# Refilling the first expert's first weight buffer in two halves, in a mixed attention, convolution and expert layer

## The chip, the cores and the metric

The kernel runs on one core of a Trainium2 chip. Its engines work side by side: TensorE (PE, with weight loads as PEld), VectorE (DVE), ScalarE (ACT), GpSimd (POOL) and SyncE (SP), which issues nearly all transfers from memory. The metric is the device time of one execution in microseconds, lower is better; the times stated are medians of several executions.

## What is computed

The reference is one encoder layer on 512 tokens of width 1024 in float32. The first half (attention heads beside a convolution, then a norm) comes first; the change lies in the second half, the mixture of experts:

```python
def expert_choice_moe(h, w_router, w_gate, w_up, w_down):
    capacity = CAPACITY_FACTOR * S // N_EXPERTS
    logits = jnp.einsum('bsd,de->bse', h, w_router).astype(jnp.float32)
    affinity = jax.nn.softmax(logits, axis=-1)
    gates, idx = lax.top_k(affinity.transpose(0, 2, 1), capacity)
    xg = jax.vmap(lambda hb, ib: hb[ib])(h, idx)
    a = jnp.einsum('becd,edf->becf', xg, w_gate)
    u = jnp.einsum('becd,edf->becf', xg, w_up)
    y = jnp.einsum('becf,efd->becd', jax.nn.silu(a) * u, w_down)
    y = y * gates[..., None].astype(y.dtype)
    ...
```

There are 16 experts, each takes its 64 best tokens (capacity 2 * 512 / 16) and has three weight matrices of 1024 x 2048 numbers, 8 MB each. The weights of all experts, some 400 MB, are read once.

## The kernel before

**Weights and memory.** A chunk is 1 MB of weights (128 rows by 2048). Expert e has 24 chunks: 0 to 7 of w_gate, 8 to 15 of w_up, 16 to 23 of w_down. Chunks live in ten buffers of 2 MB (`b` in the profile, `big_tile`), each of two slots (`s`). The first 22 chunks are loaded while the layer's first half still computes: twenty of them into slots, in the order of `first_chunks`, and chunks 14 and 15 into small tiles (`sq`, `q`) that are not part of the ring. All later chunks come in pairs: `take_big` gives the next buffer of the ring, one transfer of 2 MB fills it (L157, the function `stream`), and it waits until the products that read the buffer's old chunks are done. The first buffer holds chunks 0 and 1 and gets chunks 22 and 23, the second holds 8 and 9 and gets the first two of expert 1, and so on. SyncE issues them in this order.

**The products.** For each expert the loop of L1177 goes through blocks (k, j): k = 0 for w_gate, 1 for w_up, and j = 0 to 3 for two chunks each. Expert 0 goes (0,0), (1,0), (0,1), (1,1), (0,2), (1,2), (0,3), (1,3); the others finish k = 0 first. Within a block x and y give the chunk c = 2j + a and the half b of its columns. One such step is two matmuls in the program and four passes in the trace, since a float32 product runs as two passes; where the row of the trace says x8, that is one chunk. Steps with k = 0 are called slots. After each block `stream` issues one refill (L1249). The (1,3) block of expert 0 reads the small tiles and has no refill behind it. Then come the transposes of the hidden values (L1258) and the down products (`py`, L1287), with a refill after every second chunk.

**Other work among the products.** For expert 0 the gathered tokens `xg` are made on the way. `gather` makes them column by column: eight passes of TensorE into half a PSUM bank (`sg`, L1044), then ScalarE copies them out (L1045, 128x128). Two columns share one tile of PSUM, so columns 2 and 3 do. The loop asks for the next column at the first step of each chunk with k = 0 (L1199). `ranks` works out the places of expert e + 2 in steps taken at every third slot (L1212): a transpose (L238) that VectorE compares into masks (L240), and counts of the masks by TensorE (L245) one step later. TensorE keeps the order in which the program is written; the other engines are ordered by a scheduler.

Of the kernel before, what the change touches and what calls it, by code (L numbers as in the profile page):

```python
# [26 lines left out]
PREFETCH, LATE = 22, 14  # L27
# [19 lines left out]
def layer_kernel(ctx, tc, x, positions, emb_ln_g, emb_ln_b, w_in, q_norm_g, w_qb, kv_norm_g, w_kvb,  # L47
                 conv_w, conv_b, conv_ln_g, conv_ln_b, w_o, ln1_g, ln1_b, w_router,
                 w_gate, w_up, w_down, ln2_g, ln2_b, rope_rows, out):
    nc = tc.nc  # L50
# [22 lines left out]
    def slot(i, dt=F32):  # L73

        if (i, dt) not in handles:
            handles[i, dt] = nc.alloc_sbuf_tensor_at(f"s{len(handles)}", [128, 2048], dt,
                                                     offset=base + place[i] * 8192)
        return handles[i, dt].ap()

    def big_tile(b):  # L80
        if b not in handles:
            handles[b] = nc.alloc_sbuf_tensor_at(f"b{b}", [128, 4096], F32, offset=base + b * 16384)
        return handles[b].ap()

    def quarters(t):
        return [t[:, j * 512:(j + 1) * 512] for j in range(4)]
# [10 lines left out]
    w_tiles = {}  # L97
    next_chunk = [0]
# [4 lines left out]
    def take_big(back=True):  # L103

        b = ring.pop(0)
        if back:
            ring.append(b)
        return big_tile(b)

    def quarter_tile(q, dt=F32):  # L110
        return slots.tile([128, S], dt, name=f"q{q}")
# [4 lines left out]
    def source(i, n):  # L116

        e, r = divmod(i, 24)
        k, c = divmod(r, 8)
        if k < 2:  # L120
            rows = (w_gate, w_up)[k][0, e, c // 2 * 256:c // 2 * 256 + 256, :]
            v = rows.rearrange("(p a) n -> p a n", a=2)
            return v[:, c % 2:c % 2 + n, :]
        rows = w_down[0, e, c // 2 * 512:c // 2 * 512 + 512, :]
        v = rows.rearrange("(p a m) n -> p a (m n)", a=2, m=2)
        return v[:, c % 2:c % 2 + n, :]

    def stream(upto):
        while next_chunk[0] < min(upto, E * 24):

            n = next_chunk[0]
            if n < PREFETCH - 2:
                i = first_chunks[n]
                t = slot(first_ring[n])
                nc.sync.dma_start(t, source(i, 1)[:, 0])
                w_tiles[i] = quarters(t)
                next_chunk[0] += 1
            elif n < PREFETCH:
                i = LATE + n - PREFETCH + 2
                w_tiles[i] = []  # L140
                tiles = [quarter_tile(q) for q in range(4)] if i > LATE else [pair_tile(F32), pair_tile(F32)]
                m = 2048 // len(tiles)
                for q, t in enumerate(tiles):
                    t = t if i > LATE else t.rearrange("p a n -> p (a n)")
                    nc.sync.dma_start(t, source(i, 1)[:, 0, q * m:(q + 1) * m])
                    w_tiles[i] += [t[:, f * 512:(f + 1) * 512] for f in range(m // 512)]
                next_chunk[0] += 1
            else:
                t = take_big().rearrange("p (a n) -> p a n", a=2)
                if n == E * 24 - 2:  # L150

                    src = source(n, 2)
                    for q in range(4):
                        h = slice(q % 2 * D, q % 2 * D + D)
                        nc.sync.dma_start(t[:, q // 2, h], src[:, q // 2, h])
                else:
                    nc.sync.dma_start(t, source(n, 2))  # L157
                for a in range(2):
                    w_tiles[n + a] = quarters(t[:, a])
                next_chunk[0] += 2  # L160


    ints = slot(17, I32)
# [98 lines left out]
    with ExitStack() as pre:  # L262
# [126 lines left out]
        for c in range(DC):  # L389
            p = bank("tr")  # L390
# [149 lines left out]
        for j in range(2):  # L540
            p = project(QR + j * 128)
# [20 lines left out]
        for j in range(3):  # L562
            p = project(j * 128)
# [52 lines left out]
        for r in range(2):  # L616
            e, o = (quarters(slot(4 - 2 * r + s, F32R)) for s in range(2))
# [37 lines left out]
        for i in range(4):  # L655
            p = bank()
# [479 lines left out]
    def ranks(e):  # L1136

        pr = ps.tile([128, 512], F32, name="tr")
        ms = []
        for t in range(TT + 1):  # L1140
            if t:
                count(t - 1, pr[:, 256:256 + TT], ms[t - 1])
            if t < TT:
                ms.append(mask_tile(wk, 2))
                compare(e, t, pr[:, t % 2 * 128:(t % 2 + 1) * 128], ms[t])
            yield
        rank(e, pr[:, 256:256 + TT])

    def step(gen):
        next(gen, None)  # L1150

    hot, chosen = {}, {}
    nothing = iter(())
    ga = gather(0)
    next(ga)
    sc = nr = nothing
    for e in range(E):
# [5 lines left out]
        else:  # L1163

            order = [(k, j) for j in range(DC // 2) for k in range(2)]
        rk = ranks(e + 2) if e + 2 < E else nothing
        if e == 2:
            residual()
        left = slots_seen = 0
# [7 lines left out]
        for k, j in order:  # L1177
            p = pgu[k]
            i = 24 * e + 8 * k + 2 * j
            ws = [w_tiles.pop(i + a) for a in range(2)]  # L1180
            final = k == 1 and j == DC // 2 - 1
            if last and (k, j) == (1, 0):

                py = ps.tile([128, 512], F32, name="py")
                for t in range(TT):
                    for hf in range(2):
                        tensor(nc.tensor.matmul(py[hf * 64:(hf + 1) * 64], hot[E // 2 - 1][:, t, CAP:],
                                         acc[t][:, hf * 512:(hf + 1) * 512], start=t == 0, stop=False))
            if (k, j) == (1, 2) and s and not last:
                ga = gather(pair + 1)  # L1190
                next(ga)
            for x in range(2):
                for y in range(2):

                    a, b = (y, x) if final else (x, y)
                    c = 2 * j + a
                    if e == 0 and k == 0 and b == 0:

                        next(ga, None)  # L1199
                    for g in range(2):  # L1200
                        tensor(nc.tensor.matmul(p[b][g * 64:(g + 1) * 64, :], xg[:, c, s * CAP:(s + 1) * CAP], ws[a][2 * b + g],  # L1201
                                         start=c == 0, stop=c == DC - 1))
                    if last:
                        if k == 0 and y and left:
                            step(sc)
                            left -= 1
                    elif k and not final and left > 1:
                        step(sc)
                        left -= 1
                    elif k == 0:  # L1210
                        if slots_seen % 3 == 0:
                            step(rk)  # L1212
                        slots_seen += 1
                if final:
                    if last:
                        nc.vector.scalar_tensor_tensor(hh[:, x], sg[:, x], gate, p[x], op0=OP.mult, op1=OP.mult)
                    else:
                        nc.vector.tensor_tensor(hh[:, x], sg[:, x], p[x], op=OP.mult)  # L1218
            if (k, j) == (0, DC // 2 - 1):
                sg = pair_tile(F32)  # L1220
                hh = sg
                for b in range(2):
                    nc.scalar.activation(sg[:, b], pgu[0][b], AF.Silu)  # L1223
            if last and (k, j) == (0, DC // 2 - 1):
                nr = norm_rows()
            elif last and k and not final:
                step(nr)
                if j < 2:
                    step(nr)
            if not LATE <= i < LATE + 2:  # L1230

                if (e, k, j) == (1, 1, 3):
                    t4 = take_big(back=False)
                    acc.extend(t4[:, t * D:(t + 1) * D] for t in range(TT))
                elif (e, k, j) == (E - 2, 0, 0):

                    gb2 = take_big(back=False)
                    g2, b2 = gb2[:, :D], gb2[:, D:2 * D]
                    gb2h = quarters(gb2[:, 2 * D:])[:2]
                    spread(g2, 2 * DC, 1.0)  # L1240
                elif (e, k, j) == (E - 2, 0, 1):
                    spread(b2, 3 * DC, 1.0)
                    for dst, src in zip(gb2h, (g2, b2)):
                        for hf in range(2):
                            rs = slice(hf * 64, (hf + 1) * 64)
                            nc.scalar.activation(dst[rs], src[rs, hf * 512:(hf + 1) * 512], AF.Identity)
                    stream(next_chunk[0] + 2)
                else:
                    stream(next_chunk[0] + 2)  # L1249
# [5 lines left out]
        for b in range(2):  # L1255
            p = ps.tile([128, 512], F32, name="sg", bufs=2) if b else ps.tile([128, 512], F32, name="tr")
# [19 lines left out]
        for c in range(8):  # L1276
# [4 lines left out]
            for a in range(2):  # L1281
                f = 2 * c + a
                b, g, j = f // 8, (f // 4) % 2, f % 4
# [65 lines left out]
```

## Time and profile before

| | |
|---|---|
| median of 3 executions | 1198.47 us (1198.46 to 1198.53) |
| profiled execution, its own time | 1197.94 us |
| its span, first to last instruction | 1196.2 us |
| TensorE busy | 1122.5 us, 94% |
| VectorE, ScalarE, GpSimd busy | 380.3, 250.2, 199.3 us |
| chain that ended last | PE 65%, DMA 27% |
| read from memory | 419.60 MB |

The share of an engine is an average over the whole span. Which engine or which transfer sets the end is read from stretches: the expert stage runs from about 277 us to the end. A transfer's issue on SyncE is 0.33 us long in the trace; the data move afterwards, which the rates per stretch show.

### The profile page before, as it was taken

To read this page: it belongs to the slowest core of one execution; us is meant where nothing else is said; L and a number is where in the kernel's file an instruction comes from. 1 tells how busy PE (TensorE), PEld (TensorE's weight loads), DVE (VectorE), ACT (ScalarE), POOL (GpSimd) and SP (SyncE) were. 2 spreads that over 40 slices of the span, in tenths; PEclk is the share of its full clock that TensorE was granted. 3 is DMA by queue.
4 is the path that set the end of the run, shared out by engine and by line. 5 is a ranking of instruction groups with operands and counts; after the bars stand their busy time and mean duration, and the time that the engine had idled before them with its cause. 6 is when DMAs were issued, how large, how long until landed. Compare 5 with 4: busy or idle time off the path is not lost.

```text
span 1196.2 us, 13662 instructions
## 1 busy us (share of the span) xinstructions
PE 1122.5 (94%) x5573; PEld 529.7 (44%) x5573; DVE 380.3 (32%) x901; ACT 250.2 (21%) x461; POOL 199.3 (17%) x234
## 2 busy tenths in 40 slices
PE   4899998999999999999999999989997999899996
PEld 3687775785434343433433343324332433243422
DVE  5799998542110212122012102110311031102241
ACT  4545777322101100100110011001110101012110
POOL 6768567300000600000000000000000000000040
PEclk9899999999999999999999999999999999999998
DMA  6421014777999999999999999999999999999997
GB/s 200 138 74 43 10 68 144 253 279 292 378 425 428 428 425 427 428 428 427 428 427 428 427 427 427 428 427 427 428 428 428 428 427 427 428 427 427 428 427 293
DMA packets 43681, 422.85 MB, mean 353 GB/s; under 512 B 5178, under 2 KB 13187, under 8 KB 18018
## 3 DMA queue, kind: packets, MB, share of 16 engines
q1 hardware_dynamic: 41456, 419.18, 84.5%
q10 hardware_dynamic: 2082, 2.53, 0.6%
q8 instruction: 43, 0.70, 0.2%
q0 software_dynamic: 80, 0.26, 0.1%
q14 instruction: 20, 0.16, 0.0%
HBM read 419.60 MB, written 2.36 MB: 353 GB/s over the span
## 4 chain that ended last, share of the span: by engine, by line
PE 65%; DMA 27%; DVE 4%; ACT 2%; issue 1%; POOL 1%; ACTq 0%; POOLq 0%; SPq 0%; DVEq 0%
PE gu L1201 25%; DMA b<-in_w_up_dram 15%; PE py L1287 15%; DMA b<-in_w_down_dram 9%; PE sg L1044 6%; PE pj L258 4%; PE pj L259 3%; PE pj L260 3%; PE sg L1091 2%; DVE cv L453 1%; PE st L772 1%; ACT s L227 1%; DMA s<-in_w_in_dram 1%; PE tr L1066 1%; DMA s<-in_w_o_dram 1%; PE tr L757 1%
## 5 line engine op out<-in xcount | busy, mean ns | idle before, releaser
L1201 PE MATMUL gu<-b,xg 128*64 128x512 f32 x1920 | 446.5, 600 | 28.8 <-DMA b<-in_w_up_dram 18.1
L1201 PEld LDWEIGHTS gu<-b,xg 128*64 128x64 f32 x1920 | 124.6, 136 | 267.9 <-issue 206.4
L1287 PE MATMUL py<-b,sq 128*64 128x512 f32 x976 | 227.7, 601 | 2.7 <-DMA b<-in_w_down_dram 2.6
L1056 POOL COPY sq<-oh 128x256 f32<-128x256 f32 x16 | 6.0, 402 | 746.2 <-PE sg L1258 746.2
L1287 PEld LDWEIGHTS py<-b,sq 128*64 128x64 f32 x976 | 63.2, 136 | 106.3 <-issue 94.0
L1081 DVE SCALAR_TENSOR_TENSOR q<-py,gates,q 64x512 fp32r<-64x512 f32 x30 | 22.5, 749 | 236.3 <-ACT q L1080 236.3
L1044 PEld LDWEIGHTS sg<-oh,h 128*128 128x128 f32 x512 | 65.3, 197 | 45.5 <-issue 43.8
L258 PE MATMUL pj<-s,s 128*128 128x512 f32 x189 | 77.9, 421 | 7.6 <-ACT q L435 3.2
L1044 PE MATMUL sg<-oh,h 128*128 128x128 f32 x512 | 76.5, 293 | 1.3 <-DVE oh L1035 0.7
L259 PE MATMUL pj<-s,s 128*128 128x512 f32 x189 | 76.8, 407 | 0.0
L1218 DVE TENSOR_TENSOR sq<-sq,gu 128x512 f32<-128x512 f32 x30 | 20.6, 687 | 174.9 <-PE gu L1201 174.9
L1094 DVE TENSOR_TENSOR b<-sg,b 128x512 f32<-128x512 f32 x64 | 43.9, 690 | 83.7 <-PE sg L1091 79.6
L228 POOL TENSOR_TENSOR s<-s,s 128x512 fp32r<-128x512 f32 (+2 forms) x54 | 64.9, 1226 | 19.4 <-ACT s L227 13.0
L1262 ACT ACTIVATE sq<-tr 128x512 f32<-128x512 f32 x16 | 9.6, 597 | 273.3 <-PE tr L1258 273.3
L1045 ACT ACTIVATE xg<-sg,gbp 128x128 f32<-128x128 f32 x64 | 29.3, 458 | 162.9 <-PE sg L1044 162.9
L260 PE MATMUL pj<-s,s 128*128 128x512 f32 x157 | 63.2, 406 | 0.0
L453 DVE SCALAR_TENSOR_TENSOR cv<-s,q,cv 128x512 f32<-128x512 f32 x83 | 62.2, 749 | 1.7
L1223 ACT ACTIVATE sq<-gu 128x512 f32<-128x512 f32 x32 | 18.9, 597 | 190.6 <-PE gu L1201 190.6
L240 DVE SCALAR_TENSOR_TENSOR mask<-tr,aff,ones_b 128x128 bf16<-128x128 f32 x84 | 26.1, 348 | 102.0 <-PE tr L238 102.0
L258 PEld LDWEIGHTS pj<-s,s 128*128 128x128 f32 x189 | 37.6, 200 | 16.8 <-ACT q L435 3.7
L1091 PE MATMUL sg<-q,q 128*128 128x512 f32 (+1 forms) x128 | 44.4, 447 | 0.3 <-DVE b L1094 0.3
L259 PEld LDWEIGHTS pj<-s,s 128*128 128x128 f32 x189 | 37.2, 197 | 7.1
(287 smaller groups left out, 1076.3 us busy)
## 6 DMA issues: line engine op xcount, KB each, us to landing
b<-in_w_down_dram SPq DMA_DIRECT2D x60, 2048.0 KB, 33.8
b<-in_w_gate_dram SPq DMA_DIRECT2D x60, 2048.0 KB, 34.2
b<-in_w_up_dram SPq DMA_DIRECT2D x60, 2048.0 KB, 32.4
s<-in_w_gate_dram SPq DMA_DIRECT2D x8, 1024.0 KB, 6.6
s<-in_w_in_dram SPq DMA_DIRECT2D x12, 512.0 KB, 5.2
s<-in_w_up_dram SPq DMA_DIRECT2D x6, 1024.0 KB, 7.1
s<-in_w_down_dram SPq DMA_DIRECT2D x6, 1024.0 KB, 11.7
s<-in_w_o_dram SPq DMA_DIRECT2D x4, 1024.0 KB, 7.0
```

Of the source, the lines that this page charges most:

```text
L228: pin(eng, eng.tensor_tensor(lo, src, hi.bitcast(F32), op=OP.subtract))
L240: vector(nc.vector.scalar_tensor_tensor(mask[:, u], here, aff[:, u, e:e + 1], ones_b if u < t else before, op0=OP.is_le, op1=OP.mult, accu ...
L258: tensor(nc.tensor.matmul(p, a[0], b[0], start=start, stop=False, **kw))
L259: tensor(nc.tensor.matmul(p, a[0], b[1], start=False, stop=False, **kw))
L260: tensor(nc.tensor.matmul(p, a[1], b[0], start=False, stop=stop, **kw))
L453: nc.vector.scalar_tensor_tensor(part if k < CW - 1 else cva[j], src[k], w[k], cva[j] if k == n_act else part, op0=OP.mult, op1=OP.add)
L1044: tensor(nc.tensor.matmul(here, rows, oh[:, t, :], start=t == 0, stop=t == TT - 1))
L1045: nc.scalar.activation(xg[:, cc, :], here, AF.Identity, scale=gbp[:, 0, cc:cc + 1], bias=gbp[:, 1, cc:cc + 1])
L1091: tensor(nc.tensor.matmul(pp[h], g[h][rs, ts], parts[h][k][rs, :], start=k == 0, stop=k == 1))
L1094: nc.vector.tensor_tensor(a, pp[h], a, op=OP.add)
L1201: tensor(nc.tensor.matmul(p[b][g * 64:(g + 1) * 64, :], xg[:, c, s * CAP:(s + 1) * CAP], ws[a][2 * b + g], start=c == 0, stop=c == DC - 1))
L1287: tensor(nc.tensor.matmul(py[x * 64:(x + 1) * 64, :], hT2[:, b, j, g * 64:(g + 1) * 64], w[2 * a + hf], start=f == 0 and not last, stop=f ...
```

## The change

For expert 0 the one 2 MB transfer of chunks 22 and 23 becomes two of 1 MB (new function `stream_halves`). The first is issued when chunk 0's products are done, the second when chunk 1's are; the refill after block (0,0) falls away. To make room between the products, the gathered column that was made at chunk 1 is made at the start of block (0,1), and the ranking step of slot 0 is left out, so that each of its steps is taken three slots later.

```diff
+    def stream_halves():
+
+        n = next_chunk[0]
+        t = take_big().rearrange("p (a n) -> p a n", a=2)
+        for a in range(2):
+            nc.sync.dma_start(t[:, a], source(n + a, 1)[:, 0])
+            w_tiles[n + a] = quarters(t[:, a])
+            next_chunk[0] += 1
+            yield
...
         rk = ranks(e + 2) if e + 2 < E else nothing
+        halves_in = stream_halves() if e == 0 else nothing
...
             if (k, j) == (1, 2) and s and not last:
                 ga = gather(pair + 1)
                 next(ga)
+            if e == 0 and k == 0 and j == 1:
+                next(ga)
             for x in range(2):
                 for y in range(2):
...
-                    if e == 0 and k == 0 and b == 0:
+                    if e == 0 and k == 0 and b == 0 and c != 1:
 
                         next(ga, None)
...
                     elif k == 0:
-                        if slots_seen % 3 == 0:
+
+                        if slots_seen % 3 == 0 and (e or slots_seen):
                             step(rk)
                         slots_seen += 1
+                        if e == 0 and j == 0 and y:
+                            step(halves_in)
...
-            if not LATE <= i < LATE + 2:
+            if not LATE <= i < LATE + 2 and (e or k or j):
```

SyncE, where the first refills are issued. The words after "waits" name the counters a transfer waits for: one of eight completion counters of transfers, and TensorE's. Before:

```order
L145 DMA q_2437<-in_w_up_dram 128x512 [waits DMAHW7_49,PE_49,Activation_49]
L157 DMA b_2494<-in_w_down_dram 128x4096 [waits DMAHW0_49,PE_49]
L157 DMA b_2504<-in_w_gate_dram 128x4096 [waits DMAHW1_49,PE_49]
L157 DMA b_2532<-in_w_gate_dram 128x4096 [waits DMAHW2_49,PE_49]
L157 DMA b_2542<-in_w_gate_dram 128x4096 [waits DMAHW3_49,PE_49]
```

and now:

```order
L145 DMA q_2437<-in_w_up_dram 128x512 [waits DMAHW7_49,PE_49,Activation_49]
L167 DMA b_2475<-in_w_down_dram 128x2048 [waits DMAHW0_49,PE_49]
L167 DMA b_2475<-in_w_down_dram 128x2048 [waits DMAHW1_49,PE_49]
L157 DMA b_2494<-in_w_gate_dram 128x4096 [waits DMAHW2_49,PE_49]
L157 DMA b_2526<-in_w_gate_dram 128x4096 [waits DMAHW3_49,PE_49]
```

The first refill is two transfers of half the size into one buffer; the refills behind it keep their order.

TensorE, from the second gathered column to the first products of w_up (`gu10`, `gu11`), in which s3 is chunk 0 and s22 chunk 1. Before:

```order
L1044 MATMUL sg_2460<-oh_2453,h1_88 128x128 x3
L1201 MATMUL gu00_2456<-s3_108,xg_2454 64x512 [waits DMAHW3_49]
L1201 MATMUL gu00_2456<-s3_108,xg_2454 64x512
L238 MATMUL tr_2473<-ident_63,aff_89 128x128
L1201 MATMUL gu01_2457<-s3_108,xg_2454 64x512 x2
L1044 MATMUL sg_2479<-oh_2453,h1_88 128x128 x4
L1201 MATMUL gu00_2456<-s22_1177,xg_2454 64x512 [waits DMAHW0_49,Activation_49]
L1201 MATMUL gu00_2456<-s22_1177,xg_2454 64x512
L1201 MATMUL gu01_2457<-s22_1177,xg_2454 64x512 x2
L245 LDWEIGHTS mask_2474 [waits DVE_49]
L245 MATMUL tr_2473<-ones_b_79,mask_2474 128x1
L238 MATMUL tr_2473<-ident_63,aff_89 128x128
```

and now:

```order
L1054 MATMUL sg_2460<-oh_2453,h1_88 128x128 x3
L1214 MATMUL gu00_2456<-s3_108,xg_2454 64x512 [waits DMAHW3_49]
L1214 MATMUL gu00_2456<-s3_108,xg_2454 64x512
L1214 MATMUL gu01_2457<-s3_108,xg_2454 64x512 x2
L1214 MATMUL gu00_2456<-s22_1177,xg_2454 64x512 [waits DMAHW0_49,Activation_49]
L1214 MATMUL gu00_2456<-s22_1177,xg_2454 64x512
L1214 MATMUL gu01_2457<-s22_1177,xg_2454 64x512 x2
L248 MATMUL tr_2481<-ident_63,aff_89 128x128
```

The transpose of the first slot and the column between the two chunks are gone from here; the two chunks follow each other.

TensorE, where block (0,1) begins behind block (1,0), with s21 the last chunk of that block and s26 chunk 2. Before:

```order
L1201 MATMUL gu11_2459<-s21_1125,xg_2454 64x512 x2
L1044 MATMUL sg_2479<-oh_2453,h1_88 128x128 [waits Activation_49]
L1044 MATMUL sg_2479<-oh_2453,h1_88 128x128 x3
L1201 MATMUL gu00_2456<-s26_2052,xg_2454 64x512 x2
L1201 MATMUL gu01_2457<-s26_2052,xg_2454 64x512 x2
```

and now:

```order
L1214 MATMUL gu11_2459<-s21_1125,xg_2454 64x512 x2
L1054 MATMUL sg_2496<-oh_2453,h1_88 128x128 x4
L1054 MATMUL sg_2496<-oh_2453,h1_88 128x128 [waits Activation_49]
L1054 MATMUL sg_2496<-oh_2453,h1_88 128x128 x3
L1214 MATMUL gu00_2456<-s26_2052,xg_2454 64x512 x2
L1214 MATMUL gu01_2457<-s26_2052,xg_2454 64x512 x2
```

Columns 2 and 3 now stand one behind the other, and the second waits for ScalarE as it did before, when the first lay far ahead of it. Further on the counts of the ranking move likewise: the last four stand between blocks (0,3) and (1,3) now.

## Rows read from the trace of the kernel before

**Rows 1.** The page, the span in 40 slices: rate of transfers in each.
```profile
GB/s 200 138 74 43 10 68 144 253 279 292 378 425 428 428 425 427 428 428 427 428 427 428 427 427 427 428 427 427 428 428 428 428 427 427 428 427 427 428 427 293
```

**Rows 2.** Stretches, us from the start; last columns granted clock, DMA share, GB/s.
```profile
core 0: us, PE busy (x) PEld busy (x) DVE busy (x) ACT busy (x) POOL busy (x), PEclk, DMA share, GB/s
282.00:286.00 4.00, 4.00 (x24) 1.67 (x20) 0.17 (x2) 0.46 (x1) 0.00 (x0) 1.00 0.00 0
...
323.00:324.00 1.00, 1.00 (x8) 0.33 (x6) 0.00 (x0) 0.00 (x0) 0.00 (x0) 1.00 0.46 197
324.00:325.00 1.00, 1.00 (x6) 0.29 (x4) 0.00 (x0) 0.00 (x0) 0.00 (x0) 1.00 0.08 33
325.00:326.00 1.00, 1.00 (x6) 0.14 (x2) 0.00 (x0) 0.00 (x0) 0.00 (x0) 1.00 1.17 229
326.00:327.00 1.00, 1.00 (x12) 1.00 (x10) 0.00 (x0) 0.30 (x1) 0.00 (x0) 1.00 0.74 246
...
340.00:400.00 60.00, 59.75 (x310) 25.01 (x308) 8.29 (x32) 8.88 (x17) 7.96 (x7) 1.00 1.00 427
...
1000.00:1170.00 170.00, 158.86 (x774) 59.32 (x770) 35.30 (x77) 21.42 (x36) 14.07 (x14) 1.00 1.01 427
```

**Rows 3.** The chain that ended last, its end: start us, us, what.
```profile
1155.91 28.01 DMA b<-in_w_down_dram
```

**Rows 4.** The timeline of SyncE, refills of the ring: start, us of the issue.
```profile
285.83 0.33 SPq L157 DMA_DIRECT2D b<-in_w_down_dram  x1
289.69 0.33 SPq L157 DMA_DIRECT2D b<-in_w_gate_dram  x1
296.15 0.33 SPq L157 DMA_DIRECT2D b<-in_w_gate_dram  x1
...
314.22 0.33 SPq L157 DMA_DIRECT2D b<-in_w_up_dram  x1
324.40 0.33 SPq L157 DMA_DIRECT2D b<-in_w_up_dram  x1
329.36 0.33 SPq L157 DMA_DIRECT2D b<-in_w_up_dram  x1
```

**Rows 5.** The chain of waits at expert 0's products: start, us, what, passes.
```profile
277.52 1.20 PE sg L1044 x8
...
278.79 0.47 ACT xg L1045
...
280.51 1.01 PE gu L1201 x4
281.52 0.25 PE tr L238
...
282.78 1.14 PE sg L1044 x8
283.92 1.87 PE gu L1201 x8
...
286.06 3.58 PE gu L1201 x16
...
302.88 0.94 PE sg L1044 x8
```

**Rows 6.** The timeline of TensorE: in brackets idle time before, and its releaser.
```profile
279.30 1.21 PE L1044 MATMUL sg<-oh,h 128*128 128x128 f32 x8 [0.60 <-ACT xg L1045]
```

**Rows 7.** Timelines of TensorE and VectorE at the ranking step of slot 6.
```profile
294.80 0.30 PE L238 MATMUL tr<-ident,aff 128*128 128x128 f32 x1
...
295.96 0.08 DVE L240 DVE_READ_ACCUMULATOR mask<-tr,aff,before 128x1 f32 x1
```

**Rows 8.** Stretches as in rows 2, and TensorE's timeline: clock around idle time.
```profile
30.00:40.00 10.00, 6.66 (x29) 5.25 (x28) 4.03 (x6) 5.79 (x16) 10.00 (x13) 0.82 0.53 150
...
1165.00:1170.00 5.00, 4.33 (x20) 1.62 (x20) 1.42 (x2) 0.03 (x1) 0.00 (x0) 1.00 1.01 429
...
1165.54 3.65 PE L1201 MATMUL gu<-b,xg 128*64 128x512 f32 x16 [1.25 <-DMA b<-in_w_up_dram]
```

## The prediction

> **What bounds the kernel now.** I read the slices of the span first, then the chain of work that ended last, then fine stretches of the expert stage, and last who issued and who waited there. The transfer rate stands at 425 to 428 GB/s from the twelfth of the forty slices to the last but one [rows 1], and from 340 us to 1170 us every long stretch holds 427 to 428 GB/s [rows 2]: the weights of sixteen experts stream in without a hole. The chain ends the same way: from 1155.91 us it follows a w_down transfer of 28.01 us, and only the closing work lies behind [rows 3]. So the end is the instant from which the transfers run without a hole, plus the bytes still to come at 427 GB/s. The question is which instant that is.
>
> It is not the first refill. The list of issues shows the first refill (chunks 22 and 23, 2 MB) at 285.83 us, behind a stretch from 282 to 286 us in which nothing moves (0 GB/s) [rows 2, 4]. But the refills that follow leave only as TensorE gives memory free: 289.69, 296.15, and, after two more pairs and so on, 314.22 and then 324.40 us [rows 4]. The last step is long because the (1,3) products read the four-and-two small tiles, which are not refilled, and the down products must first use up two chunks. A refill needs 2.097 MB / 427 GB/s = 4.9 us. Seven refills stand before 324.40, 34.4 us of transfers begun at about 286 and stretched a little by waits: they are through at about 323.5. The windows show just that: the rate falls to 197 GB/s from 323 to 324 us, 33 from 324 to 325, then 229 and 246 while the refill of 324.40 sets in [rows 2]. Against 428 GB/s these four microseconds lack 231 + 395 + 199 + 182 = 1007 KB, or 2.4 us of transfers. **The queue runs empty at 324 us, and what ends that is a product of TensorE (issue at 324.40), not a transfer.** From there to the end nothing is empty again; the next issue, 329.36, comes 4.96 us later, while the one before still moves.
>
> **The change, part by part.** (1) *The two halves.* Before, chunk 0's four matmul pairs take 280.51 to 282.78 with a transpose of 0.25 us among them; then come eight gather matmuls (1.14 us) and chunk 1's products (1.87 us) to 285.79; the issue is 0.04 us later [rows 4, 5]. Now chunk 0 and chunk 1 follow each other: chunk 0's eight matmul passes end at 280.51 + 1.87 = 282.38, the first half leaves at 282.42, 3.41 us sooner; sixteen passes take 3.58 us, so the second half leaves at 284.13, 1.70 us sooner [rows 4, 5]. The second refill leaves at about 280.51 + 3.58 + 0.25 + 3.58 + 0.04 = 287.96 instead of 289.69. From the third on nothing is sooner, since all of the moved work then lies ahead of it. On the path that sets the end these 3.4 us are worth **0.00 us**: the queue is through with its first seven refills some time before 324.40 either way, and only stays empty for longer. One more issue costs SyncE 0.33 us, beside its waits of several microseconds.
>
> (2) *The moved gather.* Column 2 of the gathered tokens was made between chunks 0 and 1, column 3 seven microseconds later. Now they stand one behind the other ahead of chunk 2's products, and both lie in one tile of PSUM: the second column's matmuls wait for ScalarE to have read the first. The trace has one such pair, columns 0 and 1: matmuls at 277.52, ScalarE from 278.79 for 0.47 us, matmuls at 279.30 with 0.60 us idle, products at 280.51, so 2.99 us for the pair [rows 5, 6]. Apart, a column takes 1.14 us, the pair 2.28 [rows 5]. Cost **+0.71 us**, behind the (1,0) products, on TensorE. Nothing of another engine hides it, and the products that wait behind it are the ones that release all later memory.
>
> (3) *The moved transposes and counts.* Expert 2's ranking loses its step at the first slot and makes it up at the last: four transposes and ten counts as before, each three slots later. A run of products costs (3.58 - 1.87) / 8 = 0.214 us a pass and about 0.15 us more for being broken off and resumed (1.01 for four passes, 1.87 for eight, 3.58 for sixteen) [rows 5]. Ahead of the end of expert 0's up products there were eleven runs; now there are ten, since chunks 0 and 1 join and the last counts cut off the (1,3) products: **-0.15 us**. The last counts now have less cover: their transpose comes three slots (12 passes, 2.6 us) ahead. Vector work on a smaller step, three masks, ends 296.04 - 294.80 = 1.24 us behind its transpose, and a fourth mask adds at most a third of that, 0.41 [rows 7]: 1.65 us, which 2.6 us of products hide. Were that cover gone, TensorE would stand for those 1.65 us.
>
> (4) *The sum.* TensorE reaches the release of 324.40 later by 0.71 - 0.15 = 0.56 us; it waits for no transfer up to there, so all of it arrives. Every later transfer and the end move by the same. The profiled execution takes 1197.94 us (span 1196.2), so 1198.5; the median of the runs shown, 1198.47, lies 0.53 above it, so **1199.0 us**. The bounds: the lower one has no wait for ScalarE and merges the columns at 0.94 us, as a column behind other small matmuls takes [rows 5], that is -0.15 - 0.40 = -0.55, 1197.9; the upper one adds the whole 1.65 us of the counts, +2.21, 1200.7. I stay near the row of columns 0 and 1, the same instructions in the same tile.
>
> **The rivals.** *The head start reaches the end* (faster). If the first refill were the instant that counts, the end would come up to 3.41 us sooner, 1198.47 - 3.41 = 1195.1. For it speak the four empty microseconds from 282 to 286 [rows 2]; against it the empty queue at 324, which no earlier start can shorten. For it to hold, the drop to 33 GB/s would have to be something other than an empty queue, yet the issue of 324.40 stands right in it [rows 2, 4]. The Trainium skill (Perfetto Trace Analysis, DMA Optimizations) states such a rule: splitting transfers may let some start sooner and the whole task finish sooner where the DMA engines are generally idle. By that rule the time would be 1195.1; the trace disagrees, since from 340 us on the queues are full and the idle stretch at 324 waits for TensorE.
>
> *TensorE's clock falls* (slower). The new idle of 0.6 us lies in a stretch at full clock. Every microsecond at the lower of its two levels, 1.2 instead of 2.4 GHz, would lose half a microsecond of work, all of it ahead of 324.40. The profile has one such stretch not far from an idle TensorE: 30 to 40 us, busy 6.66 of 10 us, granted 0.82 on the mean [rows 8], so 3.6 us at the lower level and 1.8 us lost, which gives 1199.0 + 1.8 = 1200.8. Low for as long as from the stop to the issue after the (1,1) products, some 10 us, it loses 5, and 1204.0. It can be told from no change from 3.7 us at the lower level on. Against it: the same 0.60 us idle before 279.30 was followed by a clock of 1.00 from 282 to 286, and 1.25 us of idle before 1165.54 by 1.00 from 1165 to 1170 [rows 2, 6, 8]. The Trainium skill (TensorE: Matmul & The Clock Gate, The HAM clock gate) tells that idling gates this clock to half, which would be this rival; the rows beside it speak against so short a stop doing it.
>
> *The halves don't leave apart.* If each half waited for both chunks' products, the first would leave at 284.13, and the end would be the same 1199.0: only the issues would tell.
>
> **How the numbers follow.** The forecast with its bounds gets 0.88, the halves that leave together 0.03 with the same time, the head start 0.05, the clock 0.04. What a measurement can tell from no change is about 0.2%, 2.4 us, so 1196.1 to 1200.9; the forecast and its bounds lie inside. Faster by more 0.05, within 0.91, slower by more 0.04. The range is that of the bounds, 1197.9 to 1200.7, which leaves out the head start, the clock and a little more.
>
> **What would show it.** Right: two 1 MB issues at about 282.4 and 284.1 us; TensorE idle 0.6 us for ScalarE between two gather columns near 289 us; an issue near 325.0 with the rate near zero just ahead of it, for longer than before; DMA at 427 GB/s from there; the end about half a microsecond later. Wrong: an issue well ahead of 324.4 at that place, no empty queue there, a granted clock below 1 between 290 and 325 us, or an idle of TensorE ahead of the last counts.

## The result and the profile after

| | before | after |
|---|---|---|
| median of four executions each, on one chip | 1198.47 us | 1207.39 us |
| lowest and highest of them | 1193.98 to 1198.53 us | 1204.66 to 1208.37 us |
| ratio, with its 95% interval | | 1.0081 [1.0060, 1.0102] |
| profiled execution, its own time | 1197.94 us | 1206.64 us |
| its span | 1196.2 us | 1204.5 us |
| issue that was 324.40 us [rows 4] | 324.40 us | 332.87 us |

The change makes the kernel 0.8% slower, about 9 us. (The ratio is estimated from all executions; that of the two medians alone is 1.0074.) The forecast was 1199.0 us, between 1197.9 and 1200.7, with 0.91 for no change, so it was wrong.

The first place to look is TensorE's timeline at the first products of the expert stage. The columns are start, length, engine, line, operation, passes, and in brackets the idle time before and what ended it. Kernel after:

```profile
277.44 1.18 PE L1054 MATMUL sg<-oh,h 128*128 128x128 f32 x8 [0.73 <-DVE oh L1045]
279.22 1.21 PE L1054 MATMUL sg<-oh,h 128*128 128x128 f32 x8 [0.60 <-ACT xg L1055]
280.36 1.94 PE L1214 MATMUL gu<-s,xg 128*64 128x512 f32 x8
287.49 3.68 PE L1214 MATMUL gu<-s,xg 128*64 128x512 f32 x8 [5.20 <-DMA b<-in_w_down_dram]
291.11 0.48 PE L248 MATMUL tr<-ident,aff 128*128 128x128 f32 x1
291.51 4.42 PE L1214 MATMUL gu<-s,xg 128*64 128x512 f32 x16
295.86 1.21 PE L1054 MATMUL sg<-oh,h 128*128 128x128 f32 x8
297.62 1.21 PE L1054 MATMUL sg<-oh,h 128*128 128x128 f32 x8 [0.55 <-ACT xg L1055]
```

Chunk 0's products are the eight passes at 280.36, chunk 1's the eight at 287.49. Between them TensorE stands for 5.20 us, and a transfer of w_down ends the wait. Neither chunk holds w_down: the transfer is the first half of the refill, chunk 22. The chain of waits (start, length, what) goes through the same transfer, and SyncE's timeline shows it as the first of two issues on the new line L167; the others there are the refills that were issued at 296.15, 324.40 and 329.36 before [rows 4], except the one of 295.97, which answers to 289.69:

```profile
280.43 1.89 PE gu L1214 x8
282.32 0.02 issue
282.34 5.02 DMA b<-in_w_down_dram
287.36 0.14 issue
287.49 3.68 PE gu L1214 x8
```

```profile
282.34 0.33 SPq L167 DMA_DIRECT2D b<-in_w_down_dram  x1
291.21 0.33 SPq L167 DMA_DIRECT2D b<-in_w_down_dram  x1
295.97 0.33 SPq L157 DMA_DIRECT2D b<-in_w_gate_dram  x1
304.17 0.33 SPq L157 DMA_DIRECT2D b<-in_w_gate_dram  x1
...
332.87 0.33 SPq L157 DMA_DIRECT2D b<-in_w_up_dram  x1
337.83 0.33 SPq L157 DMA_DIRECT2D b<-in_w_up_dram  x1
```

The first half leaves at 282.34 us, as forecast (282.4); it takes 5.02 us to land, and chunk 1's products start 0.14 us later. The second half, forecast for 284.1, leaves at 291.21, since chunk 1's products have to end first.

The products behind the stop are slow too. In the timeline of before the same eight passes took 1.94 us, the sixteen of the next block 3.65; now they take 3.68 and 4.42. The stretches show why; the third number from the end is the granted clock, the last one the transfer rate in GB/s:

```profile
282.00:287.00 5.00, 0.30 (x2) 0.00 (x0) 0.00 (x0) 0.00 (x0) 0.00 (x0) 0.93 0.64 210
...
287.00:293.00 6.00, 5.51 (x13) 1.57 (x15) 0.36 (x2) 0.00 (x0) 0.00 (x0) 0.50 0.13 23
293.00:296.00 3.00, 3.00 (x15) 0.84 (x12) 0.00 (x0) 0.00 (x0) 0.00 (x0) 0.98 0.82 303
...
331.00:332.00 1.00, 1.00 (x6) 0.37 (x8) 0.00 (x0) 0.00 (x0) 0.00 (x0) 1.00 0.24 98
332.00:333.00 1.00, 1.00 (x6) 0.29 (x4) 0.00 (x0) 0.00 (x0) 0.00 (x0) 1.00 0.08 33
333.00:334.00 1.00, 1.00 (x8) 0.28 (x4) 0.00 (x0) 0.00 (x0) 0.00 (x0) 1.00 0.66 115
334.00:335.00 1.00, 1.00 (x10) 0.53 (x6) 0.00 (x0) 0.00 (x0) 0.00 (x0) 1.00 0.64 164
340.00:400.00 60.00, 60.00 (x308) 24.71 (x304) 7.59 (x29) 7.55 (x15) 0.00 (x0) 1.00 1.00 425
```

The clock fell while TensorE stood (0.93 is the mean from 282 to 287 us). From 287 to 293 us it is 0.50, the lower of its two levels, and from about 293 it is back. The four rows from 331 to 335 us answer to the four microseconds around 324 us of before [rows 2]: again the rate falls to 33 GB/s and the issue, now of 332.87, stands right in it. From 340 us on 425 GB/s flow. The list of waits adds up what TensorE waited for in the whole stretch from 270 to 600 us (us in total, times, longest). Its two largest entries:

```profile
PE gu L1214 <- DMA b<-in_w_down_dram: 5.2, 1, 5.2
PE sg L1054 <- ACT xg L1055: 1.1, 2, 0.6
```

One wait for the half, and two for ScalarE: the pair of columns 0 and 1 as before, and 0.55 us for the new pair. The list has one wait for a mask of the ranking, 0.5 us, but it lies ahead of the first gather matmul and stands in before too; the moved ranking steps wait for no mask.

### The profile page after: what moved, and what is told of

Read it like the earlier page. It is cut to its first block, busy times and chain, and to the rows that moved or that the text cites. A ratio compares the mean times of both kernels' runs of the same rounds, so it can differ in the third digit from the quotient of the medians.

```text
span 1204.5 us, 13664 instructions
## 1 busy us (share of the span) xinstructions
PE 1125.9 (93%) x5573; PEld 530.6 (44%) x5573; DVE 386.0 (32%) x901; ACT 250.1 (21%) x461; POOL 199.2 (17%) x234
## 4 chain that ended last, share of the span: by engine, by line
PE 65%; DMA 27%; DVE 4%; ACT 2%; issue 1%; POOL 1%; ACTq 0%; POOLq 0%; SPq 0%; DVEq 0%
PE gu L1214 25%; DMA b<-in_w_up_dram 15%; PE py L1303 15%; DMA b<-in_w_down_dram 9%; PE sg L1054 6%; PE pj L268 3%; PE pj L269 3%; PE pj L270 3%; PE sg L1101 2%; DVE cv L463 1%; PE st L782 1%; ACT s L237 1%; DMA s<-in_w_in_dram 1%; PE tr L1076 1%; DMA s<-in_w_o_dram 1%
```

## The experiments

All runs are compared with the kernel before on the same chip. The work ahead of the expert stage takes a few microseconds more or less from one execution to the next, whatever the kernel, so beside the ratio the table gives the *tail*, from the start of the first gather matmul (277.52 us in before [rows 5]) to the end of the span, in the one profiled execution. In the nine kernels in which the refill of 324.40 us or the one behind it sets the end by the count below, 871.3 to 871.9 us lie between the issue of the first of the two and the end of the span. So the end follows this issue, and a difference of less than about 0.6 us in a tail tells nothing.

The last column is a count that I formed only after half of the runs, and on which two later runs were forecast. For each refill it takes the issue, from the first gather matmul on, less 2.4515 us for every MB of refills that was ordered before it (1.0486 MB at 427.7 GB/s, between the 427 and 428 of the long stretches [rows 1]). Where the queue has run empty, that difference is the time that has been lost by then, and the largest over all refills should set the end. In before it is 12.55 for the issue of 324.40 us (46.87 - 14 x 2.4515), 12.61 for 329.36, then 11.79 and 11.83 for issues at 397.18 and 421.74 us, and falls from there on: at most 6.8 from 450 us.

| kernel | ratio [95%] | tail, us | against before | by the count |
|---|---|---|---|---|
| before | | 918.65 | | |
| after | 1.0081 [1.0060, 1.0102] | 927.09 | +8.44 | +8.55 |
| e1_slots | 1.0015 [1.0002, 1.0027] | 918.61 | -0.04 | +0.48 |
| e2_late_halves | 1.0003 [0.9988, 1.0018] | 919.00 | +0.35 | +0.48 |
| e3_kept_busy | 1.0050 [1.0029, 1.0070] | 924.50 | +5.85 | +5.89 |
| e7_halves_alone | 1.0067 [1.0042, 1.0092] | 924.77 | +6.12 | +6.32 |
| e8_moved_alone | 0.9994 [0.9977, 1.0011] | 919.22 | +0.57 | +0.47 |
| e4_delay_early | 1.0025 [1.0008, 1.0043] | 920.66 | +2.01 | +2.23 |
| e5_delay_late | 1.0027 [1.0007, 1.0048] | 920.77 | +2.12 | +1.45 |
| e6_down_slots | 1.0008 [0.9995, 1.0021] | 919.35 | +0.70 | -0.78 |
| e9_delay_fourth | 0.9995 [0.9981, 1.0010] | 918.71 | +0.06 | 0.00 |
| e10_delay_more | 1.0020 [1.0004, 1.0036] | 920.87 | +2.22 | +2.51 |

**What makes chunk 1 wait?** The theory: the half is written through the name of the whole 2 MB buffer, and what orders reads behind writes takes that buffer as one piece, so that chunk 1, which lies in its other half and isn't touched, counts as written. The first run names the two halves apart.

```diff
-        t = take_big().rearrange("p (a n) -> p a n", a=2)
+        b = ring.pop(0)
+        ring.append(b)
         for a in range(2):
-            nc.sync.dma_start(t[:, a], source(n + a, 1)[:, 0])
-            w_tiles[n + a] = quarters(t[:, a])
+            t = slot(pairs[b][a])
+            nc.sync.dma_start(t, source(n + a, 1)[:, 0])
+            w_tiles[n + a] = quarters(t)
```

> The changed kernel with one thing altered: the two halves are written through the two 1 MB slots that chunks 0 and 1 were loaded through, not through the 2 MB buffer that covers both. Theory A (chunk 1's products wait for the first half to land, because the buffer is tracked as one piece): that wait is gone, TensorE's longest idle there is the 0.6 us for ScalarE, the clock stays 1.00, the refill that was at 324.40 us leaves at about 324.9, and the time is 0.5 us over before (ratio 1.0004). Rival B (two transfers of 1 MB, or the shifted turn of the eight completion counters, slow the stream): still about 8 us over before. Rival C (the moved gather and counts cost it): still about 8 us over. Rival D (an earlier first refill does reach the end once the wait is gone): 3.4 us under before (0.997).

TensorE's timeline of this run, and SyncE's first three refills:

```profile
280.33 1.21 PE L1056 MATMUL sg<-oh,h 128*128 128x128 f32 x8 [0.60 <-ACT xg L1057]
281.47 3.65 PE L1216 MATMUL gu<-s,xg 128*64 128x512 f32 x16
285.05 0.32 PE L250 MATMUL tr<-ident,aff 128*128 128x128 f32 x1
```

```profile
283.44 0.33 SPq L169 DMA_DIRECT2D s<-in_w_down_dram  x1
285.16 0.33 SPq L169 DMA_DIRECT2D s<-in_w_down_dram  x1
289.00 0.33 SPq L157 DMA_DIRECT2D b<-in_w_gate_dram  x1
```

The sixteen passes of chunks 0 and 1 run through, and the halves leave 4.90 and 6.61 us behind the first gather matmul (278.55 us here), where before one transfer left after 8.31. This is the change as the prediction took it to be, and its tail is that of before (the 1.0004 that was expected lies in the interval of its ratio). The 3.41 us of head start bring nothing that can be told: the eighth refill leaves 47.35 us behind the first gather matmul, as in the run further down that has the moved work without the halves (47.34). The built programs say the same of the cause: chunk 1's first matmul waits until its transfer counter stands at 112 in before and in this run, and at 160 in the changed kernel, which is the value that the first half brings it to.

The second run keeps the whole buffer's name and puts both halves behind chunk 1.

```diff
-                        if e == 0 and j == 0 and y:
+                        if e == 0 and j == 0 and x and y:
+                            step(halves_in)
                             step(halves_in)
```

> The changed kernel, but both halves are issued behind chunk 1's products, through the 2 MB buffer as in the change. Theory A: chunk 1's products stand ahead of the first half in the program and wait for nothing new; 0.5 us over before. Rival B (halves as such): about 8 us over. Rival C (moved work): about 8 us over.

Tail +0.35 us, no stop. So two 1 MB transfers into one named buffer cost nothing that the tail can tell; what costs is a read of the other half behind the first.

**Which part of the change is it?** One run leaves the gathered column and the ranking step where they were and only splits the refill; another one moves the work and keeps the single refill.

```diff
-            if e == 0 and k == 0 and j == 1:
-                next(ga)
...
-                    if e == 0 and k == 0 and b == 0 and c != 1:
+                    if e == 0 and k == 0 and b == 0:
...
-                        if slots_seen % 3 == 0 and (e or slots_seen):
+                        if slots_seen % 3 == 0:
```

> The two halves through the 2 MB buffer, but the gathered column and the ranking steps where they stood before. Theory A: chunk 0 ends at 282.8, the first half lands 5.0 us later, the column between hides 1.1 us, TensorE idles 3.9 us; with a falling clock 5 to 7 us over before (1.004 to 1.006), 3.9 (1.003) if the clock holds. Rival C (moved work is the cause): no difference from before.

```diff
-                        if e == 0 and j == 0 and y:
-                            step(halves_in)
...
-            if not LATE <= i < LATE + 2 and (e or k or j):
+            if not LATE <= i < LATE + 2:
```

> The gathered column and the ranking steps moved as in the change, the first refill one 2 MB transfer behind block (0,0) as before. Theory A: only the 0.7 us of the pair of columns less 0.15, so 0.5 us over before (1.0004). Rival C (moved work is the cause of the loss): about 8 us over before.

The place of the stop with the halves alone, and the place of the pair with the moved work alone, both from TensorE's timeline:

```profile
279.61 1.21 PE L1054 MATMUL sg<-oh,h 128*128 128x128 f32 x8
284.94 3.68 PE L1212 MATMUL gu<-s,xg 128*64 128x512 f32 x8 [4.12 <-DMA b<-in_w_down_dram]
```

```profile
284.28 1.21 PE L1054 MATMUL sg<-oh,h 128*128 128x128 f32 x8
286.04 1.21 PE L1054 MATMUL sg<-oh,h 128*128 128x128 f32 x8 [0.55 <-ACT xg L1055]
```

The halves alone cost 6.12 us, the moved work 0.57. Where the gather column stands between the chunks, it hides 1.1 us of the half's transfer, and the stop is 4.12 instead of 5.20 us. The change therefore took from between the chunks the work that would have covered part of the wait that it made. That is part of why the two costs add up to 6.69 us and not to 8.44: 1.08 us of the rest is the longer stop; what makes up the other 0.7 was not measured by itself.

**How much is the stop, how much the clock?** The next run is the changed kernel with nineteen matmuls, whose result nobody reads, at the place of the stop.

```diff
+    def busy(n):
+
+        p = ps.tile([128, 512], F32, name="sg", bufs=2)
+        for _ in range(n):
+            tensor(nc.tensor.matmul(p[:, :128], ident, ident, start=True, stop=True))
...
                             step(halves_in)
+                            if not x:
+                                busy(19)
```

> The changed kernel with 19 matmuls of 128x128 between chunk 0 and chunk 1 whose result nobody reads (38 passes at 0.122 us, 4.6 us), which lie inside the 5.2 us wait. Theory A with the clock as its second part: the wait for the first half ends at the same time, but TensorE's clock stays 1.00, so that the 2.9 us of products at half clock are not lost: 5.7 us over before (1.0048). If the clock is not part of it: 8.3 us over as the changed kernel (1.007), or more by the added work.

TensorE's timeline, then the stretches as above:

```profile
281.03 4.51 PE L1163 MATMUL sg<-ident 128*128 128x128 f32 x38
286.30 1.94 PE L1220 MATMUL gu<-s,xg 128*64 128x512 f32 x8 [0.76 <-DMA b<-in_w_down_dram]
288.16 0.32 PE L248 MATMUL tr<-ident,aff 128*128 128x128 f32 x1
288.42 3.65 PE L1220 MATMUL gu<-s,xg 128*64 128x512 f32 x16
```

```profile
286.00:290.00 4.00, 3.71 (x17) 1.33 (x19) 0.36 (x2) 0.00 (x0) 0.00 (x0) 1.00 0.25 45
290.00:300.00 10.00, 9.45 (x52) 4.66 (x50) 0.63 (x4) 1.37 (x3) 0.00 (x0) 1.00 0.80 298
```

Chunk 1's products start 10.05 us behind the first gather matmul in both (286.30 - 276.25 here, 287.49 - 277.44 in after), so the wait is the same, but the clock stays at 1.00 and the products take 1.94 and 3.65 us. The tail is 2.59 us shorter than that of the changed kernel. That is the price of the clock.

**Does TensorE's lateness reach the end, and from how far?** The next two runs are the kernel before with ten such matmuls ahead of the block of chunks 2 and 3, once in the first expert and once in the second.

```diff
             p = pgu[k]
+            if (e, k, j) == (0, 0, 1):      # (1, 0, 1) in the second run
+                busy(10)
```

> The kernel before with 10 matmuls of 128x128 ahead of expert 0's block (0,1), whose result nobody reads: 20 passes, 2.4 us, and 0.15 us for the break, on TensorE ahead of the refill of 324.40 us. If that refill, at the empty queue, sets the end: 2.6 us over before (1.0022). If the end is set by the first refill (285.83 us, ahead of the added work): no difference.

> The kernel before with the same 10 matmuls ahead of expert 1's block (0,1), near 340 us, behind the refill of 324.40 us. If the transfers run without a hole from 324.40 on: less than 0.3 us over before. If TensorE's work sets the end everywhere: 2.6 us over (1.0022).

The early delay came out at +2.01 us, where 2.6 were expected. The late one did not: +2.12 instead of less than 0.3, although its issue of the eighth refill stands where it stood, 46.87 us behind the first gather matmul. The stretches of this run, 116 to 124 and 128 to 132 us behind the first gather matmul, show new holes; at the same distance before had 426 and 434 GB/s in the first two and 438 in the third:

```profile
389.50:393.50 4.00, 3.75 (x24) 1.75 (x24) 1.86 (x4) 2.92 (x6) 3.26 (x3) 1.00 0.98 381
393.50:397.50 4.00, 4.00 (x22) 1.31 (x20) 0.63 (x4) 0.00 (x0) 4.00 (x4) 1.00 0.97 389
...
401.50:405.50 4.00, 4.00 (x25) 1.34 (x24) 1.51 (x10) 0.00 (x0) 4.00 (x4) 1.00 0.95 340
```

This is where I formed the count. The refills of 397.18 and 421.74 us are only 0.8 us better off than the one that sets the end, so a delay of 2.2 us makes them the latest: 14.06, or +1.45.

Another run tried to shorten the empty stretch at 324 us. The first four down chunks of expert 0 are refilled one by one, through the names of the slots.

```diff
-            if c % 2:
+            if e == 0 and c < 4:
+                stream_slot()
+            elif c % 2:
                 stream(next_chunk[0] + 2)
```

> The kernel before, with the refills of expert 0's first four down chunks issued one chunk at a time through slots of 1 MB (four 1 MB transfers behind chunks 16, 17, 18 and 19 instead of two of 2 MB behind 17 and 19). If the empty queue at 324 us sets the end: the first of them leaves at about 321.1 us, the 2.4 us of missing transfers shrink to under 0.5, and the time is 2 us under before (0.998). If the first refill sets the end: no difference.

Nothing was gained (+0.70 us). The first of these issues stands 43.63 us behind the first gather matmul, 3.24 sooner, but with 1 MB on order at a time the rate stays low for longer. The last number again, from 324 us on (47.7 us behind the first gather matmul), where before had 332, 393, 438 and 414 GB/s at the same distance:

```profile
324.00:328.00 4.00, 4.00 (x28) 2.05 (x24) 0.16 (x1) 0.60 (x1) 0.00 (x0) 1.00 1.04 367
328.00:332.00 4.00, 4.00 (x22) 1.38 (x20) 0.00 (x0) 0.00 (x0) 0.00 (x0) 1.00 0.94 369
332.00:336.00 4.00, 4.00 (x19) 1.14 (x15) 0.26 (x1) 0.68 (x1) 0.00 (x0) 1.00 1.01 365
336.00:340.00 4.00, 4.00 (x21) 1.34 (x22) 2.14 (x8) 0.68 (x1) 0.00 (x0) 1.00 0.95 365
```

The count, which knows only how much is on order, would have given -0.78, up to the refill of 421.74. It doesn't explain the 365 to 369 GB/s. Why the rate is lower with single chunks on order, I leave open.

Two last runs put the count to the test, against the simpler rule that TensorE sets the end as long as it waits for no transfer. They are the delay in the fourth expert, with ten and with forty matmuls.

> The kernel before, with the same ten added matmuls (nobody reads their result; 2.2 us of TensorE) ahead of the block of chunks 2 and 3 of the fourth expert, some 173 us behind the first gather matmul. Theory: of each refill count its issue, from the first gather matmul on, less the 2.45 us per MB that the refills ahead of it take; the largest of these sets the end. In the kernel before the largest is 12.61 us (issue of 329.36 us), and from the place of the new matmuls on none is over 6.8. With 2.2 us more they stay at 9.0, so the end does not move: less than 0.3 us from the kernel before, counted from the first gather matmul, ratio 1.000. Rival: TensorE's work sets the end as long as TensorE waits for no transfer, which it first does some 330 us behind the first gather matmul; then the end is later by 2.0 to 2.6 us, as with the same matmuls in the first and the second expert, ratio 1.002.

> As the run before with forty matmuls instead of ten in the same place, 8.9 to 9.6 us of TensorE. Theory: the refills behind them reach 6.2 + 9.2 = 15.4 us, 2.8 over the 12.61 that set the end before, so the end is 2 to 3.5 us later, ratio about 1.0023. Rival (TensorE's work sets the end up to its first wait for a transfer): 9 us later, ratio 1.0075. If neither end moves, refills that far behind have more in hand than the count tells.

```profile
449.49 2.40 PE L1153 MATMUL sg<-ident 128*128 128x128 f32 x20
```

```profile
450.04 9.10 PE L1153 MATMUL sg<-ident 128*128 128x128 f32 x80
```

The first fence is the timeline of ten matmuls (twenty passes), the second of forty. The 2.40 us leave no trace at the end (+0.06 us), and of the 9.10 us only 2.22 arrive, where the count gives 2.51 and the rule 9. With forty the stretches show the hole that has opened (320 and 328 GB/s), with ten there is none:

```profile
460.50:464.50 4.00, 4.00 (x23) 1.15 (x19) 0.90 (x6) 0.00 (x0) 0.00 (x0) 1.00 0.90 320
464.50:468.50 4.00, 4.00 (x24) 1.34 (x24) 1.58 (x11) 0.00 (x0) 0.00 (x0) 1.00 0.84 328
```

```profile
460.00:464.00 4.00, 4.00 (x24) 1.37 (x22) 0.86 (x2) 0.96 (x2) 0.00 (x0) 1.00 1.00 426
464.00:468.00 4.00, 4.00 (x22) 1.29 (x18) 0.00 (x0) 0.24 (x1) 0.00 (x0) 1.00 1.02 426
```

Of the eleven changed kernels none is faster than before beyond its interval.

## Why the prediction was wrong, point by point

**The step that failed** is in (4): "it waits for no transfer up to there, so all of it arrives". That holds for the kernel before. In the changed kernel TensorE does wait for one, the first half of the refill itself, for 5.20 us. In (1) the prediction had written that "chunk 0 and chunk 1 follow each other", and it priced the issue of the half but not who reads the buffer afterwards. The order of the instructions shows the wait of chunk 1's first matmul as "waits DMAHW0_49,Activation_49" before and after, word for word, and I read that as the same wait. The counter is the same, the value is not (112 and 160). The question to ask was what writes the memory last, in program order, ahead of that read. e1 and e2 show the cause from two sides.

**The size of it.** The release that was 46.87 us behind the first gather matmul is at 47.35 in e1, at 52.76 in e3 and at 55.42 in the changed kernel. So the moved work is 0.48, the stop 5.41 (TensorE idle for 5.20 of it in the changed kernel), and the lower clock 2.66 us, together the 8.55 by which the release is late; the tail is 8.44 late.

**The moved gather and ranking, (2) and (3).** These were right. The new pair waits 0.55 us for ScalarE, with 0.60 taken from the pair of columns 0 and 1 [rows 6]; the sum of 0.56 us met 0.47 to 0.48 in the releases of e1, e2 and e8. The last counts wait for nothing.

**The first refill's head start, (1).** It is worth nothing that can be told, as said, when it happens. In e1 the halves leave 3.41 and 1.70 us sooner, the very numbers of the prediction, and the tail stays at -0.04. So the head start, as a rival, falls: the idle stretch from 282 to 286 us [rows 2] has no price. The Trainium skill (Perfetto Trace Analysis, DMA Optimizations) says that splitting transfers may let the whole task finish sooner where the DMA engines are generally idle. Here they are idle from 282 to 286 us but not in general (427 GB/s from 340 us on [rows 2]). A transfer did start 3.41 us sooner and the task did not end sooner, since the idle time that counts, at 324 us, waits for TensorE.

**The clock rival** had 0.04. Its mechanism came, its trigger did not: after the forecast stop of 0.55 us the clock is at 1.00 (e8 has no slow product behind it), and it fell in the stop of 5.20 us that I hadn't seen. Its price of half a microsecond for each at the lower level fits: the 5.51 us of work at 0.50 would lose 2.8, and 2.6 were measured.

**The bound at 324 us.** That TensorE's release there sets the end held for every delay ahead of it (after, e3, e4, e7): the time from that release to the end stayed within 871.5 and 871.8 us. What follows it, "from there to the end nothing is empty again", was read rightly off the rates and taken for more than it says. A full queue doesn't tell how near it is to running empty. The next late refills are 0.8 us behind the first; e5 and e6 were mis-forecast for want of that number, e9 and e10 were forecast with it. It is a rough tool all the same: it misses e5 by 0.7 and e6 by 1.5 us.

## What to carry to other kernels

When a transfer into part of a buffer moves ahead of a read of another part, ask which name the write goes through: if it is that of the whole buffer, the reader waits for the transfer to land, and the list of instructions may show the same counter with only another value. Give each part its own name, or issue the transfer behind the last read. To see which refill sets the end, subtract from each issue the time that the bytes ordered before it need. By this count the largest difference is the bound, and the gap to the next one is the most that a cure at that place can bring. The added delays bear out the first, roughly; the second is not shown, since e6 gained nothing.

## What the runs showed of the hardware

A stop of TensorE of 5.20 us was followed by some 6 us at a granted clock of 0.50, and one of 4.12 us (e7) by the same level from 285 to 289 us, as the stretch of that run below shows; the stops of 0.55, 0.60 and 0.76 us left it at 1.00. The 5.20 us stop cost another 2.6 us in this way, half as much again. The Trainium skill (TensorE: Matmul & The Clock Gate, The HAM clock gate) tells that idling gates the clock to half; these runs agree for the long stops.

```profile
285.00:289.00 4.00, 4.00 (x12) 0.98 (x12) 0.00 (x0) 0.00 (x0) 0.00 (x0) 0.50 0.00 0
```

One chunk of 1 MB, issued to queues that were empty, took 5.02 us until it landed, while in the stream of 2 MB refills each MB takes 2.45 us (428 GB/s). Whoever waits for a single transfer pays the longer time.
